# Prompt attention of a hybrid encoder layer: the probability-times-value products turned round, on two column halves of the array, four tiles at a time

## Chip, cores, metric

One core of one Trainium2 chip. The metric is the device time of one execution in microseconds (us). Engines: PE is TensorE (PEld its weight loads), DVE is VectorE, ACT is ScalarE, POOL is GpSimd, SP is SyncE, which here only issues DMAs.

## What is computed

The kernel computes one encoder layer for two token batches with shared weights, a prompt of 1024 tokens (called A in the code, `T.n` = 8 blocks of 128) and a sample of 512 (called B, `T.n` = 4). A layer has an RMS norm, one wide input projection, a bidirectional mLSTM branch, a dilated window attention branch, and two output projections. The change is in the attention branch alone, cut here to its core:

```python
A_PATTERNS = ((128, 1), (512, 4), (2048, 16))     # (window, dilation), 3 groups x 8 heads x 64
# per group: keys gathered by stride, blocks of 64 queries, 128 + 64 keys in the window
logits = einsum('bghnqe,bghnke->bghnqk', qr, kb) + bias
logits = where(mask, logits, -inf)
mx = max(logits, -1); p = exp(logits - mx[..., None]); den = sum(p, -1)
o = einsum('bghnqk,bghnke->bghnqe', p, vb)        # unnormalised
# the three groups are then mixed, weighted by exp(mx) and den
```

## The kernel before

The program runs in stages: projections of A, mLSTM of A, attention of A, mLSTM of B beside the mix of A's groups, attention of B, and the last projections. From the mLSTM of A on, the order of instructions on PE and on SP is the order in which the code issues them; on DVE, ACT and POOL a scheduler sets it at build time, by the times that it computes. Each engine executes its instructions in that order.

Between its own steps each of these stages issues dense products of another part of the layer. They come from `Fill` (L116); `fill(1)` issues about the next share of them. Their weights are loaded by DMA into `wraw` (in the attention of A by POOL), split by ACT into a high part `wh` (L274) and by DVE into a low part `wl` (L280), and multiplied in three passes by `mm3` (L211 to L213). `split_w` puts these splits behind the last attention steps in `self.held`.

Attention works on one pair of heads of one group at a time: `attend` (L1429) goes through 12 such pairs, and `attention` (L1322) cuts each into `n` tiles of 128 queries. There are three kinds of tiles. In groups 0 and 1 (dilations 1 and 4) of the prompt a tile has two key blocks of 128 (`nk` = 2), 44 tiles in all; at the ends of a sequence two half tiles of 64 queries are put together, each with one key block (`ends`, 20 tiles); in group 2 a tile has one key block (32 tiles). That makes 96 tiles for A.

A tile has four steps. `products` (L1366) multiplies queries and keys into the PSUM bank `lg`. `softmax` adds the bias and takes the maximum on DVE (L1386), negates it (L1388), and takes exponentials on ACT, with their sums (L1390). `turn` transposes the probabilities on PE into the bank `pt` (L1397) and copies them to `pts` in SBUF, on ACT (L1400) for every second tile, on DVE (L1402) for the others. `output` (L1405) multiplies: the weights of the array are the 128 x 128 probabilities, and 64 columns of values stream, for each head and key block (L1418; in an end tile the values of both blocks stream as 128 columns, L1411). The result has queries on partitions; ACT copies it from the bank `o` into the row buffer `ot` (L1420, L1414), which also holds the sums and maxima in columns 128 to 131 (`OW` = 132), and `put` (L217) queues the DMA store to `og`, issued on SP three rounds later by `tick` (L233).

The steps of consecutive tiles are interleaved. A round, `att_round` (L1490), issues these, `age` being how many rounds ago a tile began:

```python
for age, stage in ((0, 0), (1, 1), (2, 2), (None, None), (3, 3)):
    if age is None:
        fill(1)
    elif age < len(tiles) and tiles[-1 - age] is not None:
        tiles[-1 - age][stage]()
```

So PE gets, in each round: `lg` of the newest tile, transposes of the one two rounds older, dense products, and the PV products of the one three rounds older. All operands of the PV products are plain f32. `Rot` (L92) hands out row buffers in turn: ten `ot` for A. Each PSUM bank name has two buffers.

Of the kernel before, what the change touches and what calls it, by code (L numbers as in the profile page):

```python
# [22 lines left out]
F32 = mybir.dt.float32  # L23
F32R = mybir.dt.float32r
AF = mybir.ActivationFunctionType
# [4 lines left out]
P = 128  # L30
D = 1024
KT = D // P
BLK = 512
# [10 lines left out]
OW = 132  # L44
# [139 lines left out]
class Net:  # L184
# [1137 lines left out]
    def attention(self, T, u, qkv, bias, sb, ps):  # L1322

        nc = self.nc
        g, pr = divmod(u, 4)
        S, n, dil = T.S, T.n, min(DILS[g], T.n)
        L = S // dil
        wide = L > P
        W = 256 if wide else P
        q, k, v = qkv  # L1330
        c0 = 128 * (pr % 2)

        def table(c):
            b = bias()[:, :2 * W].rearrange("p (h w) -> p h w", h=2)
            j = 8 * CASES.index((g, dil)) + 2 * pr
            for hh in range(2):
                e = self.erow[j + hh]
                self.queue(("table", u), None, b[:, hh],
                           bass.AP(tensor=e.tensor, offset=e.offset + 257 - c - W, ap=[[1, P], [1, W]]))
            return b[:, :, ::-1]  # L1340


        og = T.og[:, g, pr]
        tiles, H = [], 64
        early, late = slice(H, P), slice(0, H)
# [12 lines left out]

        def stages(turned, qp, kp, kt, bt, dst, ends):
            nk = 1 if ends else len(kt)  # L1360
            W = nk * P
            pair = slice(kt[0], kt[-1] + 1, max(kt[-1] - kt[0], 1))
            qs = slice(qp, qp + P)
            ts = {}

            def products():  # L1366
                lg = self.bank("lg")
                if wide:
                    ts["lg"] = [lg[:, 0], lg[:, 1]]
                    for hh in range(2):  # L1370
                        for z in (k[hh], k[2 + hh]):
                            nc.tensor.matmul(lg[:, hh], q[hh][:, qs], z.rearrange("p (n j) -> p n j", j=P)[:, pair],  # L1372
                                             start=z is k[hh], stop=z is not k[hh])
                else:
                    kk = [z[:, kt[0]].rearrange("p a j -> p (a j)") for z in k]
                    ts["lg"] = [lg[:, 0, :P], lg[:, 0, P:2 * P]]
                    self.mm3(lg[:, 0], (q[0][:, qs], q[1][:, qs]), kk, True, True)

            def softmax():
                ls = ts["ls"] = sb.tile([P, 2, W], F32, name="ls", bufs=3)  # L1380
                ot = ts["ot"] = self.ot()
                nm = sb.tile([P, 2], F32, name="nm", bufs=3)
                blocks = [(late, slice(P, 2 * P), slice(0, P)), (early, slice(0, P), slice(P, 2 * P))]
                for hh in range(2):
                    for rows, of, by in blocks if ends else [(slice(0, P), slice(0, W), slice(0, W))]:
                        nc.vector.tensor_tensor_reduce(out=ls[rows, hh], in0=ts["lg"][hh][rows, of], in1=bt[rows, hh, by], scale=1.0,  # L1386
                                                       scalar=NEG, op0=OP.add, op1=OP.max, accum_out=ot[rows, 130 + hh:131 + hh])
                nc.vector.tensor_scalar(nm, ot[:, 130:132], -1.0, None, op0=OP.mult)  # L1388
                for hh in range(2):
                    self.held = self.held[-3:] + [nc.scalar.activation(ls[:, hh], ls[:, hh], AF.Exp, bias=nm[:, hh:hh + 1],  # L1390
                                                                      accum_out=ot[:, 128 + hh:129 + hh])]

            def turn():
                pp = self.bank("pt")
                for hh in range(2):
                    for x in range(nk):
                        nc.tensor.transpose(pp[:, hh * nk + x], ts["ls"][:, hh, x * P:(x + 1) * P], self.ident)  # L1397
                pt = ts["pt"] = sb.tile([P, 4, P], F32, name="pts", bufs=2)[:, :2 * nk]
                if turned:
                    last = nc.scalar.activation(pt, pp[:, :2 * nk], AF.Copy)  # L1400
                else:
                    last = nc.vector.tensor_copy(pt, pp[:, :2 * nk])  # L1402
                self.held = self.held[-3:] + [last]

            def output():  # L1405
                pt, ot = ts["pt"], ts["ot"]
                po = self.bank("o").rearrange("p a b -> p (a b)")
                vh = lambda x, hh: v[:, x, c0 + hh * 64:c0 + hh * 64 + 64]
                if ends:
                    for hh in range(2):  # L1410
                        nc.tensor.matmul(po[:, hh * P:hh * P + P], pt[:, hh], vh(pair, hh), start=True, stop=True)  # L1411
                    by = po[:, :2 * P].rearrange("p (h x e) -> p h x e", h=2, x=2)
                    for x, rows in enumerate((early, late)):
                        last = nc.scalar.activation(ot[rows, :128].rearrange("p (h e) -> p h e", h=2), by[rows, :, x], AF.Copy)  # L1414
                else:
                    for hh in range(2):
                        for x in range(nk):
                            nc.tensor.matmul(po[:, hh * 64:hh * 64 + 64], pt[:, hh * nk + x], vh(kt[x], hh), start=x == 0,  # L1418
                                             stop=x == nk - 1)
                    last = nc.scalar.activation(ot[:, :128], po[:, :128], AF.Copy)  # L1420
                self.held = self.held[-3:] + [last]
                for p0, cnt, row, stp in dst:
                    self.put(("og", S), og[row:row + (cnt - 1) * stp + 1:stp], ot[p0:p0 + cnt], ot)

            return products, softmax, turn, output

        return [stages(i % 2, *x) for i, x in enumerate(tiles)]

    def attend(self, T, fill, steps, first, banks, outs, after=None, beside=None, at=()):  # L1429

# [2 lines left out]
        nc = self.nc  # L1433
        self.lag = 3
        with ExitStack() as st:
# [3 lines left out]
            make = lambda b: ps.tile(shape[b], F32, name=b, bufs=2)  # L1439
            spare = {b: make(b) for b in banks}  # L1440
            self.bank = lambda b: spare.pop(b) if b in spare else make(b)
            self.ot = Rot(self, [sb.tile([P, OW], F32, name=f"ot{i}", bufs=1) for i in range(outs)])
            tables = self.pool(st, "bias" + T.name, 1, "right")
            bias = Rot(self, [tables.tile([P, BLK], F32, name=f"bias{i}", bufs=1) for i in range(4)])
            if T.n > 4:
                tables.tile([P, 2560], F32, name="apart", bufs=1)
            tiles = []
            fill.stage(steps, 12 * T.n)

# [12 lines left out]
            for i in range(12):  # L1462
                now = coming
                for j, t in enumerate(now):
# [13 lines left out]
                    self.att_round(tiles, fill)  # L1478
                    if len(tiles) in at:
                        next(beside, None)  # L1480
            for _ in range(3):
                self.tick()
                tiles.append(None)
                self.att_round(tiles, fill)
# [4 lines left out]

    def att_round(self, tiles, fill):  # L1490

        for age, stage in ((0, 0), (1, 1), (2, 2), (None, None), (3, 3)):
            if age is None:
                fill(1)
            elif age < len(tiles) and tiles[-1 - age] is not None:
                tiles[-1 - age][stage]()


# [269 lines left out]
STEPS = (316, 260, 192, 290, 86)  # L1768


def body(tc, a):
    N = Net(tc, a)
    nc = tc.nc
    (x1, y1), (x2, y2) = a["runs"]
    with ExitStack() as st:
# [145 lines left out]
        with ExitStack() as s1:  # L1921
# [30 lines left out]
            def hold(name, make):  # L1952
                def go():
                    kept[name] = make()
                return go

            with ExitStack() as s2:
# [11 lines left out]
                with ExitStack() as s3:  # L1969
                    N.gate_sums(B, N.pool(s3, "sums", 1, "right"))  # L1970
                    lanes = N.lanes(B, N.pool(s3, "lane2", 1, "right"), lambda: N.bank("o").rearrange("p a b -> p (a b)"), True)
                    N.attend(A, fill, STEPS[1], kept["qkv"], ("pt", "o", "lg"), 10, hold("head", lambda: N.ml_load(B, 0)),
                             lanes, range(44, 96, 8))
                    for _ in lanes:
                        pass
                    N.close()
# [90 lines left out]
```

## Time and profile before

| | us |
|---|---|
| median of 3 executions | 2236.45 |
| lowest, highest | 2235.32, 2239.72 |
| profiled execution, its time | 2236.86 |
| profiled execution, its span | 2235.1 |
| granted TensorE clock, mean | 0.998 |
| PE busy | 2218.1 (99%) |
| DVE busy | 1523.7 (68%) |
| ACT busy | 1120.3 (50%) |
| POOL busy | 715.7 (32%) |

In the profile each instruction has a start and a length. Lengths of PE's products overlap, since a product's results leave the array while the next one streams; how long a product holds the array is read from the distance between two starts. In a group, "xN" is the number of records, and a plain f32 product has two records, a float32r one has one. After `|` stand busy time, the mean of one in ns and idle time before it, with what ended it; in a timeline that stands in square brackets. The shape behind a product's name is first rows * columns of the weights, then what streams (partitions x columns).

### The profile page before, as it was taken

The numbers are of one execution on the slowest core, as the hardware profiler recorded it, in microseconds if no ns is written. First come the engines' busy times: TensorE is split into PE (matmuls) and PEld (weight loads), VectorE is DVE, ScalarE is ACT, GpSimd is POOL, SyncE is SP. The second block draws the span as 40 slices with busy tenths as digits, with TensorE's granted clock in tenths as the row PEclk, the third lists the DMA queues.
The fourth block names the chain that finished last, engine by engine and source line by source line (L and its number), as shares of the span: only waits on it lengthen the run. The fifth ranks groups of instructions, "written<-read, shape, count | busy, mean of one in ns | idle before, by whom it ended". The sixth has DMA issues, their size and how long they took to land.

```text
span 2235.1 us, 34988 instructions
## 1 busy us (share of the span) xinstructions
PE 2218.1 (99%) x11962; PEld 1939.6 (87%) x11962; DVE 1523.7 (68%) x2989; ACT 1120.3 (50%) x2394; POOL 715.7 (32%) x988
## 2 busy tenths in 40 slices
PE   9999999999999999999999999999999999999998
PEld 8999888888888888888888889989888888888887
DVE  7775667687776665558887765555689855665674
ACT  7332343344444343456776655656666644554332
POOL 1000423333333222236677620011165522221221
PEclk9999999999999999999999999999999999999999
DMA  3742444433323223385754779997678887776663
GB/s 124 192 115 81 174 155 165 165 141 113 113 105 112 85 85 122 114 279 173 236 186 157 191 200 247 260 250 210 208 242 289 259 261 236 236 255 201 232 233 113
DMA packets 217661, 408.81 MB, mean 183 GB/s; under 512 B 24938, under 2 KB 128042, under 8 KB 217483
## 3 DMA queue, kind: packets, MB, share of 16 engines
q1 hardware_dynamic: 187784, 298.51, 42.7%
q0 software_dynamic: 26096, 95.47, 13.7%
q10 hardware_dynamic: 3602, 12.59, 1.4%
q8 instruction: 95, 1.56, 0.3%
q14 instruction: 84, 0.68, 0.1%
HBM read 286.75 MB, written 119.73 MB: 182 GB/s over the span
## 4 chain that ended last, share of the span: by engine, by line
PE 94%; issue 2%; DMA 2%; DVE 1%; ACT 1%; POOL 0%; SPq 0%; DVEq 0%; POOLq 0%; ACTq 0%
PE d L213 14%; PE d L211 14%; PE d L212 14%; PE dense L211 12%; PE dense L213 12%; PE dense L212 12%; PE o L1418 3%; PE pt L1397 2%; PE lg L1372 2%; PE num L213 1%; PE num L211 1%; PE num L212 1%; PE a L1088 1%; PE kv L211 1%; PE kv L212 1%
## 5 line engine op out<-in xcount | busy, mean ns | idle before, releaser
L211 PE MATMUL dense<-H,wh 128*128 128x512 f32 x664 | 270.3, 407 | 0.0
L213 PE MATMUL dense<-H,wl 128*128 128x512 f32 x664 | 260.6, 392 | 0.0
L212 PE MATMUL dense<-H,wh 128*128 128x512 f32 x664 | 260.4, 392 | 0.0
L212 PE MATMUL d<-Hl,phla 128*128 128x512 f32 x608 | 236.5, 389 | 0.0
L213 PE MATMUL d<-Hh,phla 128*128 128x512 f32 x608 | 236.5, 389 | 0.0
L211 PE MATMUL d<-Hh,phla 128*128 128x512 f32 x608 | 236.5, 389 | 0.0
L280 DVE TENSOR_TENSOR wl<-wraw,wh 128x1024 fp32r<-128x1024 f32 (+1 forms) x121 | 150.0, 1240 | 72.8 <-ACT wh L274 72.5
L1386 DVE CUSTOM_DVE_ANT_0 ls<-lg,bias 128x256 f32<-128x256 f32 (+2 forms) x336 | 103.0, 332 | 116.5 <-PE lg L1372 55.4
L211 PE MATMUL d<-Hh,phlb 128*128 128x512 f32 x456 | 177.4, 389 | 0.0
L212 PE MATMUL d<-Hl,phlb 128*128 128x512 f32 x456 | 177.4, 389 | 0.0
L213 PE MATMUL d<-Hh,phlb 128*128 128x512 f32 x456 | 177.4, 389 | 0.0
L1390 ACT ACTIVATE ls<-ls,nm 128x128 f32<-128x128 f32 (+1 forms) x288 | 124.8, 435 | 92.7 <-DVE nm L1388 58.9
L274 ACT ACTIVATE wh<-wraw 128x1024 fp32r<-128x1024 f32 (+1 forms) x124 | 128.5, 1036 | 77.0 <-PE dense L212 26.1
L213 PEld LDWEIGHTS dense<-H,wl 128*128 128x128 f32 x664 | 124.7, 188 | 28.0
L695 POOL TENSOR_TENSOR psum_w<-pw_raw 128x512 f32<-128x512 f32 x38 | 58.5, 1540 | 278.4 <-DMA pw_raw<-w_in 259.6
L213 PE MATMUL d<-vhi,Hl 128*128 128x322 f32 x448 | 140.5, 314 | 0.5 <-DVE Hl L431 0.3
L211 PE MATMUL d<-vhi,Hh 128*128 128x322 f32 x448 | 140.3, 313 | 0.1
L212 PE MATMUL d<-vlo,Hh 128*128 128x322 f32 x448 | 139.6, 312 | 0.0
L212 PEld LDWEIGHTS dense<-H,wh 128*128 128x128 f32 x664 | 125.3, 189 | 14.3
L211 PEld LDWEIGHTS dense<-H,wh 128*128 128x128 f32 x664 | 125.1, 188 | 14.4
L213 PEld LDWEIGHTS d<-Hh,phla 128*128 128x128 f32 x608 | 114.2, 188 | 23.7
L211 PEld LDWEIGHTS d<-Hh,phla 128*128 128x128 f32 x608 | 114.2, 188 | 23.6
(574 smaller groups left out, 6105.0 us busy)
## 6 DMA issues: line engine op xcount, KB each, us to landing
pw_raw<-w_in SPq DMA_DIRECT2D x76, 512.0 KB, 4.1
wraw<-w_in SPq DMA_DIRECT2D x64, 512.0 KB, 4.6
aqk_a<-pwk SPq DMA_DIRECT2D x48, 512.0 KB, 3.5
aqk_b<-sw SPq DMA_DIRECT2D x48, 256.0 KB, 6.2
wraw<-w_pm POOLq DMA_DIRECT2D x24, 512.0 KB, 6.0
wraw<-w_out POOLq DMA_DIRECT2D x24, 512.0 KB, 3.9
wraw<-w_v POOLq DMA_DIRECT2D x22, 430.0 KB, 6.9
qk_a<-pwk SPq DMA_DIRECT2D x16, 512.0 KB, 2.7
```

The costliest lines, as they stand in the source:

```text
L211: nc.tensor.matmul(out, lh, rh, start=start, stop=False, **kw)
L212: nc.tensor.matmul(out, lh, rl, start=False, stop=False, **kw)
L213: nc.tensor.matmul(out, ll, rh, start=False, stop=stop, **kw)
L274: high = nc.scalar.activation(hi[:, :n], raw[:, :n], AF.Copy)
L280: low = (self.lows or nc.vector).tensor_sub(lo[:, :n], raw[:, :n], hi[:, :n].bitcast(F32))
L695: self.nc.gpsimd.tensor_add(s[:, 0], ws[1][:, 0], ws[1][:, 1])
L1088: nc.tensor.matmul(p[:, c - c0], kT[:, ct, c * P:(c + 1) * P], qT[:, ct, c * P:(c + 1) * P], start=ct == 0, stop=ct == 1)
L1372: nc.tensor.matmul(lg[:, hh], q[hh][:, qs], z.rearrange("p (n j) -> p n j", j=P)[:, pair], start=z is k[hh], stop=z is not k[hh])
L1386: nc.vector.tensor_tensor_reduce(out=ls[rows, hh], in0=ts["lg"][hh][rows, of], in1=bt[rows, hh, by], scale=1.0, scalar=NEG, op0=OP.add, op ...
L1390: self.held = self.held[-3:] + [nc.scalar.activation(ls[:, hh], ls[:, hh], AF.Exp, bias=nm[:, hh:hh + 1], accum_out=ot[:, 128 + hh:129 + hh])]
L1397: nc.tensor.transpose(pp[:, hh * nk + x], ts["ls"][:, hh, x * P:(x + 1) * P], self.ident)
L1418: nc.tensor.matmul(po[:, hh * 64:hh * 64 + 64], pt[:, hh * nk + x], vh(kt[x], hh), start=x == 0, stop=x == nk - 1)
```

## The change

For the prompt alone (`by_four`, `n > 4`) the PV products are turned round. The weights are now 64 columns of values, and the 128 columns of transposed probabilities stream; the output has the 64 channels of a head on partitions. Head 0 writes to partitions 0 to 63 and so uses columns 0 to 63 of the array, head 1 uses the other half of both. The products of four consecutive tiles are issued together, in `columns`, in the round in which the fourth tile's `output` stood, into one bank `o`. One ACT copy brings the bank to SBUF (`oT`); in the next round, behind that round's `lg` products and transposes and ahead of its dense products, `back` transposes the four tiles on PE into a bank `pt`, one ACT copy brings them to the row buffer, and the four tiles' stores are queued together. A row buffer holds four tiles, and there are four of them instead of ten; `pts` has six buffers instead of two; one closing round is added. An end tile uses four products with 64 streaming columns each instead of two. The sample's attention is unchanged. A spacer tile `apart` in SBUF shrinks.

```diff
+        by_four = n > 4
...
             def softmax():
                 ls = ts["ls"] = sb.tile([P, 2, W], F32, name="ls", bufs=3)
-                ot = ts["ot"] = self.ot()
+                if not by_four:
+                    ot = ts["ot"] = self.ot()
+                else:
+                    if slot == 0:
+                        batch["of"] = self.ot()
+                    ot = batch["of"].rearrange("p (t w) -> p t w", w=OW)[:, slot]
...
-                pt = ts["pt"] = sb.tile([P, 4, P], F32, name="pts", bufs=2)[:, :2 * nk]
+                pt = ts["pt"] = sb.tile([P, 4, P], F32, name="pts", bufs=6 if by_four else 2)[:, :2 * nk]
+                batch[slot] = (pt, kt, ends, dst)
...
+            def columns():
+                if slot < 3:
+                    return
+                po = self.bank("o").rearrange("p a b -> p (a b)")
+                vh = lambda x, hh: v[:, x, c0 + hh * 64:c0 + hh * 64 + 64]
+                for t in range(4):
+                    pt, kt, ends, _ = batch[t]
+                    of = lambda hh, a, b: po[hh * 64:hh * 64 + 64, t * P + a:t * P + b]
+                    for x in range(len(kt)):
+                        for hh in range(2):
+                            if ends:
+                                a, b = ((H, P), (0, H))[x]
+                                nc.tensor.matmul(of(hh, a, b), vh(kt[x], hh), pt[:, hh, a:b], start=True, stop=True)
+                            else:
+                                nc.tensor.matmul(of(hh, 0, P), vh(kt[x], hh), pt[:, hh * len(kt) + x], start=x == 0,
+                                                 stop=x == len(kt) - 1)
+                oT = batch["oT"] = sb.tile([P, BLK], F32, name="oT", bufs=2)
+                self.held = self.held[-3:] + [nc.scalar.activation(oT, po, AF.Copy)]
+
+            def back():
+                if slot < 3:
+                    return
+                pb = self.bank("pt")
+                for t in range(4):
+                    nc.tensor.transpose(pb[:, t], batch["oT"][:, t * P:(t + 1) * P], self.ident)
+                of = batch["of"]
+                ot = of.rearrange("p (t w) -> p t w", w=OW)
+                self.held = self.held[-3:] + [nc.scalar.activation(ot[:, :, :P], pb, AF.Copy)]
+                for t in range(4):
+                    for p0, cnt, row, stp in batch[t][3]:
+                        self.put(("og", S), og[row:row + (cnt - 1) * stp + 1:stp], ot[p0:p0 + cnt, t], of)
+
+            if by_four:
+                return products, softmax, turn, columns, back
             return products, softmax, turn, output
...
-            self.ot = Rot(self, [sb.tile([P, OW], F32, name=f"ot{i}", bufs=1) for i in range(outs)])
+            self.ot = Rot(self, [sb.tile([P, (4 if T.n > 4 else 1) * OW], F32, name=f"ot{i}", bufs=1) for i in range(outs)])
...
-                tables.tile([P, 2560], F32, name="apart", bufs=1)
+                tables.tile([P, 640], F32, name="apart", bufs=1)
...
-            for _ in range(3):
+            for _ in range(4 if T.n > 4 else 3):
...
-        for age, stage in ((0, 0), (1, 1), (2, 2), (None, None), (3, 3)):
+        for age, stage in ((0, 0), (1, 1), (2, 2), (4, 4), (None, None), (3, 3)):
```

More of the change, by code (lines that the diff above doesn't have):

```diff
@@ L1357, in attention, with stages @@
                 tiles.append((t * P, t * P, (t,), b0, [(0, P, t, dil)], False))
-        def stages(turned, qp, kp, kt, bt, dst, ends):
+        def stages(turned, slot, batch, qp, kp, kt, bt, dst, ends):
             nk = 1 if ends else len(kt)
@@ L1423, in output @@
                     self.put(("og", S), og[row:row + (cnt - 1) * stp + 1:stp], ot[p0:p0 + cnt], ot)
+            def columns():
[30 more added lines that the diff above has]
+                return products, softmax, turn, columns, back
             return products, softmax, turn, output
-        return [stages(i % 2, *x) for i, x in enumerate(tiles)]
+        batches = [{} for _ in range(n // 4)]
+        return [stages(i % 2, i % 4, batches[i // 4], *x) for i, x in enumerate(tiles)]
     def attend(self, T, fill, steps, first, banks, outs, after=None, beside=None, at=()):
@@ L1490, in att_round @@
     def att_round(self, tiles, fill):
-        for age, stage in ((0, 0), (1, 1), (2, 2), (None, None), (3, 3)):
+        for age, stage in ((0, 0), (1, 1), (2, 2), (4, 4), (None, None), (3, 3)):
             if age is None:
                 fill(1)
-            elif age < len(tiles) and tiles[-1 - age] is not None:
+            elif age < len(tiles) and tiles[-1 - age] is not None and stage < len(tiles[-1 - age]):
                 tiles[-1 - age][stage]()
@@ L1971, in body @@
                     lanes = N.lanes(B, N.pool(s3, "lane2", 1, "right"), lambda: N.bank("o").rearrange("p a b -> p (a b)"), True)
-                    N.attend(A, fill, STEPS[1], kept["qkv"], ("pt", "o", "lg"), 10, hold("head", lambda: N.ml_load(B, 0)),
+                    N.attend(A, fill, STEPS[1], kept["qkv"], ("pt", "o", "lg"), 4, hold("head", lambda: N.ml_load(B, 0)),
                              lanes, range(44, 96, 8))
```

## The prediction

> **What bounds the kernel now.** I read the page's busy times and its chain first, then the stage that the change touches, the prompt's attention (about 1305 to 1618 us), as one stretch of the table by stretches, then single rounds of it in the timeline of PE.
>
> ```profile
> PE 2218.1 (99%) x11962; PEld 1939.6 (87%) x11962; DVE 1523.7 (68%) x2989; ACT 1120.3 (50%) x2394; POOL 715.7 (32%) x988
> PE 94%; issue 2%; DMA 2%; DVE 1%; ACT 1%; POOL 0%; SPq 0%; DVEq 0%; POOLq 0%; ACTq 0%
> ```
> ```profile
> 1300.00:1620.00 320.00, 316.55 (x2058) 298.94 (x2057) 180.56 (x722) 200.29 (x658) 30.43 (x60) 0.99 0.88 234
> ```
> TensorE is busy for 99% of the span and is 94% of the chain. The second fence has, after the stretch and its length, the busy time of PE, PEld, DVE, ACT and POOL, the clock, the DMA share and GB/s: here too PE works 316.55 of 320 us, while ACT works 200 and DVE 181. The dense products that `fill` puts between the attention steps leave PE no gap, so a microsecond of PE time saved or added in this stage moves the end by about as much.
>
> **What a PV product costs today.** One round with two key blocks, as PE sees it (start, length, engine, line):
>
> ```profile
> 1399.68 0.36 PE L212 MATMUL dense<-wl,H 128*128 128x430 f32 x1
> 1399.88 0.36 PE L213 MATMUL dense<-wh,H 128*128 128x430 f32 x1
> 1400.07 1.00 PE L1418 MATMUL o<-K,pts 128*128 128x64 f32 x8
> 1400.88 0.36 PE L1372 MATMUL lg<-V1a,Q 128*128 128x256 f32 x1
> 1401.08 0.28 PE L1372 MATMUL lg<-V1b,Q 128*128 128x256 f32 x1
> 1401.20 0.28 PE L1372 MATMUL lg<-V1a,Q 128*128 128x256 f32 x1
> 1401.32 0.28 PE L1372 MATMUL lg<-V1b,Q 128*128 128x256 f32 x1
> 1401.44 0.60 PE L1397 MATMUL pt<-ident,ls 128*128 128x128 f32 x4
> 1401.79 0.44 PE L211 MATMUL dense<-wh,H 128*128 128x430 f32 x1
> 1402.08 0.35 PE L212 MATMUL dense<-wl,H 128*128 128x430 f32 x1
> ```
> ```profile
> L1418 PE MATMUL o<-K,pts x480: 217/275/294, 1320.1 to 1618.0; 128*128 128x64 f32 x160
> ```
> ```profile
> L1411 PE MATMUL o<-K,pts x80: 270/275/422, 1344.1 to 1528.4; 128*128 128x128 f32 x80
> ```
> Durations overlap, so I cost by starts. Each plain f32 product shows as two records, two passes over the array; the tile's four products are the "x8". From the last dense start (1399.88) to the second `lg` start (1401.08) are 1.20 us. Without the passes between, that would be one dense step (1399.68 to 1399.88, 0.20) and one `lg` step (1401.08 to 1401.20, 0.12). So eight passes cost 0.88 us, 0.11 each, although only 64 columns stream in each. The prompt's attention has 480 + 80 = 560 such passes: 560 x 0.11 = **61.6 us removed**.
>
> **The price of a turned pass.** The weights become 64 columns of `v`, and 128 columns of `pt` stream. The rate of an f32 pass is seen where 512 columns stream against narrow weights; the second row, from the groups by form, ends in the mean of one in ns:
>
> ```profile
> 184.76 1.05 PE L355 MATMUL d<-oh,tb 128*32 128x512 f32 x2
> ```
> ```profile
> L355 PE MATMUL d<-oh,tb 128*32 128x512 f32 x2 | 1.0, 604 | 0.0
> ```
> The pair takes 1.05 us and one takes 0.60, so starts are 0.45 apart: 0.11 for 128 columns, 0.055 for 64. The changed tiles have 480 passes of 128 columns (44 tiles with two blocks, 8 passes each; 32 with one block, 4 each) and 160 of 64 (20 end tiles, 8 each). One after the other that is 480 x 0.11 + 160 x 0.055 = 61.6 us: nothing saved. The change pays only if the two heads' halves stream at once. No row here shows two products side by side, so this term lies between 61.6 and about half. I take the half: 26.4 for the wide passes, 8.8 for the narrow ones, whose weights (64 columns at half the 0.11 of 128) take as long as their stream, and 0.11 x 24 batches = 2.6 for the pass that begins alone: **37.8 us added**.
>
> The Trainium skill (TensorE: Matmul & The Clock Gate, Part 3) measured three column tiles at 2.38 times one, not 3; an estimate at that efficiency makes the wide passes about 33 us instead of 26.4 and the forecast about 2250. No run here shows it.
>
> **Changing the array's division.** The only place where one narrow pair sits in a dense stream is this:
>
> ```profile
> 140.23 0.31 PE L212 MATMUL d<-vlo,Hh 128*128 128x322 f32 x1
> 140.38 0.31 PE L213 MATMUL d<-vhi,Hl 128*128 128x322 f32 x1
> 140.62 0.21 PE L981 MATMUL d<-ident,l_u 64*1 64x64 f32 x1
> 140.67 0.21 PE L982 MATMUL d<-ident,l_tt 64*1 64x64 f32 x1
> 140.81 0.42 PE L211 MATMUL d<-vhi,Hh 128*128 128x322 f32 x1
> 141.07 0.32 PE L212 MATMUL d<-vlo,Hh 128*128 128x322 f32 x1
> ```
> A dense step is 0.15. Going in takes 0.24 (0.09 more); coming out 0.14 after a stream of 0.05 (0.09 more); the first dense product then needs 0.26 (0.11 more), its weights no longer loaded in the shadow. With 0.055 for the first 64 weights, a batch pays 0.35, and 24 batches **8.4 us**. Going in and out at no cost is the lower bound.
>
> **Turning back.** In the round above four transposes (1401.44 to 1401.79) take 0.35 and push the dense step after them from 0.20 to 0.29 (1401.79 to 1402.08): 0.44. 24 batches: **10.6 us**.
>
> Array time together, with overlap: 37.8 + 8.4 + 10.6 - 61.6 = **-4.8 us**.
>
> **The wait that is new.** Today nothing on PE needs the copy behind a PV product (L1420, L1414), it only goes to the store. Now PE's transposes back need the ACT copy `oT`, one round step later, and PE is in order: the dense products of `fill(1)` stand behind them. From the start of the last column pass, `back` is reached after 0.11 (stream) + 0.09 + 0.11 (coming out) + 4 x 0.12 (`lg`) + 4 x 0.11 (turn) = 1.2 us; 1.0 if the turned tile has one block of each head, 0.9 in the third group (three `lg` steps, two transposes). The copy is ready after 0.27 (one pass of L1411) + 0.04 + 0.58 (below) = 0.9 us, if ACT is free. It often is not:
>
> ```profile
> 1398.78 0.58 ACT L1400 ACTIVATE pts<-pt 128x512 f32<-128x512 f32 x1
> ```
> ```profile
> 1320.07 1.00 PE L1418 MATMUL o<-K,pts 128*128 128x64 f32 x8
> ```
> ```profile
> 1321.10 0.28 ACT L1420 ACTIVATE ot<-o 128x128 f32<-128x128 f32 x1 [0.71 <-PE o L1418]
> ```
> ```profile
> 1486.84 0.50 PE L1411 MATMUL o<-K,pts 128*128 128x128 f32 x3
> ```
> ```profile
> 1490.79 0.92 ACT L274 ACTIVATE wh<-wraw 128x860 fp32r<-128x860 f32 x1 [5.25 <-DMA wraw<-w_v]
> 1491.74 0.56 ACT L1414 ACTIVATE ot<-o 64x128 f32<-64x128 f32 x2
> ```
> ```profile
> 1617.72 0.55 PE L1418 MATMUL o<-K,pts 128*128 128x64 f32 x4
> ```
> ```profile
> 1618.31 0.28 ACT L1420 ACTIVATE ot<-o 128x128 f32<-128x128 f32 x1 [2.02 <-PE o L1418]
> ```
> These are the first, one of the worst and the last of 96. The first copy begins 0.03 after the product's end (1321.07), the last 0.04 after it (1618.27), one of the two worst 4.40 after it (1487.34), because ACT stood 5.25 us in front of a weight split whose DMA was late. Over all 96 the lags add to about 58 us; every fourth, where a batch would end, adds to 20.9, and less a slack of 0.2 each to about 17. Five of those lie together between 1430 and 1490 and have one cause: counting only the worst, since PE's own wait lets ACT catch up, leaves about 10. I take **+10 us** (bounds 1 and 17).
>
> A wait can cost more than itself:
>
> ```profile
> 1493.57 1.19 PE L1397 MATMUL pt<-ident,ls 128*128 128x128 f32 x4 [2.07 <-ACT ls L1390]
> ...
> 1495.26 0.56 PE L213 MATMUL dense<-X,H 128*128 128x430 f32 x1
> 1495.62 0.56 PE L211 MATMUL dense<-wh,H 128*128 128x430 f32 x1
> ```
> After 2.07 us of idle PE the dense step is 0.36 instead of 0.20 for some microseconds. The Trainium skill (the same page, Part 1) puts the fall of the clock behind an idle window of about 3.4 us; the trace has it after 2.07. By the page no wait forecast here would slow the clock; by the row one or two may, which lies inside the bounds.
>
> **The smaller parts.** Three rounds of four lose their PV part, 0.88 or 0.45 us, so exponentials have less time before their transposes; the fence above holds the only long wait of this kind, so I add 1 us (0 to 3). One more closing round, with `back` right behind `oT`: about 0.7. Six `pts` buffers replace two because four tiles are held; PE waits on none. Stores are as many and as large, but four to six stand together on SP behind the round's loads. Four `ot` buffers of four tiles hold 16 tiles against 10, so a store has longer to land; I cost this at nothing, and if a load behind the burst came late, the price would be a wait like the 2.07 above. ACT gets two 0.58 copies per batch for four to six of 0.28, no work of weight.
>
> Sum: -4.8 + 10 + 1 + 0.7 = +6.9. The profiled execution took 2236.86 (span 2235.1), the median 2236.45; so **2243 us**, slower by 0.3%. From no change a measurement of this kernel can tell about 0.2%, 4.5 us.
>
> **Rivals.** (a) *Overlap, and ACT in time*: `oT` stands early enough in ACT's order, weights load in both halves at once so that the narrow passes halve too (-4.4). -4.8 - 4.4 + 1.7 gives 2229; without the second gain 2233. For it: the scheduler orders ACT anew around `oT`, and half of the 96 copies begin within 0.25 us. Against: the lags above. It decides if the waits at `back` stay under about 1 us in all. The Trainium skill (TensorEngine Tiling, Key Properties) says that different tiles load and multiply in parallel, which is this case; no row shows it. (b) *The halves run one after the other*: 61.6 + 8.4 + 10.6 - 61.6 = +19.0, some 6 of waits (ACT has longer to catch up) and 1.7: 2263. For it: f32 passes in two records per head come as a, a, b, b, and no row shows overlap. (c) *Half overlap*, if there is one spare set of weights for both halves: each pair of passes takes a stream and a load, 0.165, so 480 x 0.0825 + 11.4 = 51, +8.4 with the rest, +11.7: 2256. (d) *No load in the shadow at all*: +0.055 on all 640 passes over (b), 2298. Against it: L1418's eight passes at 0.11 each leave no room for load plus stream of 0.165. The Trainium skill (TensorE: Matmul & The Clock Gate, Part 3) has loads overlapping a running product only where the row group differs; the trace contradicts it.
>
> **Numbers.** Forecast 0.45 (2235 to 2252), (a) 0.18, (b) 0.24, (c) 0.10, (d) 0.03. Faster by over 0.2%: most of (a), 0.17. Within 0.2%: the rest of (a) and a quarter of the forecast, 0.15. Slower: 0.68. The range, 2229 to 2264, leaves out (d), the outer half of (b) and of (a).
>
> **What would show it.** In the trace after: starts of the column passes 0.055 apart on average (overlap) or 0.11 (none); 0.09 and 0.11 lost at each end of a batch; "pt<-ident,oT" idle on "ACT oT" for about 10 us in all, most of it around the late weights. I am wrong if that idle time is near nothing, or if the passes do not pair.

## The result and the profile after

The changed kernel takes 2249.48 us (median of 4 executions, 2244.92 to 2251.58) against 2235.89 before: ratio 1.0056, 95% interval 1.0035 to 1.0076. It is slower by 0.6%. The profiled execution is the shortest of the four, 2244.92 us with a span of 2243.2, so the traces show 8.1 us of difference (2235.1 to 2243.2). What the other three executions spend more, 4 to 7 us, no trace shows; the record has only their mean granted clocks, 0.996, 0.995 and 0.994 from the shortest to the longest, against 0.996 in the profiled one.

The busy times and the shares of the chain (the work that ended last, followed back from the end), from the page of the kernel after:

```profile
PE 2211.5 (99%) x12138; PEld 1918.7 (86%) x12138; DVE 1523.2 (68%) x2989; ACT 1120.1 (50%) x2326; POOL 712.4 (32%) x988
PE 87%; issue 4%; DMA 4%; ACT 1%; DVE 1%; POOL 1%; SPq 0%; DVEq 0%; POOLq 0%; ACTq 0%
```

PE works 6.6 us less than before and the span is 8.1 us longer, so PE stands still some 15 us more. Its share of the chain falls from 94% to 87%. The stretch of the attention of A in the table by stretches (stretch, length, busy time of PE, PEld, DVE, ACT, POOL, clock, DMA share, GB/s):

```profile
1300.00:1620.00 320.00, 303.30 (x2198) 272.74 (x2197) 176.23 (x717) 197.96 (x586) 29.39 (x58) 0.98 0.87 233
```

PE was busy 316.55 of these 320 us before, and now 303.30. ACT and DVE do no more work than before. The longest of PE's waits in this stage, before and after (PE's tile and line, then the engine, tile and line it waited for, us in all, times, longest):

```profile
PE pt L1397 <- ACT ls L1390: 2.1, 1, 2.1
```
```profile
PE pt L1456 <- ACT oT L1449: 16.3, 7, 6.2
```

The second is the new wait of `back` for the copy of the columns, 16.3 us. How it comes about is seen around one batch, first in the timeline of PE, then in that of ACT:

```profile
1403.63 0.35 PE L213 MATMUL dense<-wh,H 128*128 128x430 f32 x1
1403.92 1.97 PE L1446 MATMUL o<-pts,K 128*64 128x128 f32 x32
1405.81 0.39 PE L1373 MATMUL lg<-V1a,Q 128*128 128x256 f32 x1
1406.04 0.28 PE L1373 MATMUL lg<-V1b,Q 128*128 128x256 f32 x1
...
1406.39 0.60 PE L1403 MATMUL pt<-ident,ls 128*128 128x128 f32 x4
1410.02 0.66 PE L1456 MATMUL pt<-ident,oT 128*128 128x128 f32 x4 [3.02 <-ACT oT L1449]
1410.43 0.44 PE L211 MATMUL dense<-wh,H 128*128 128x430 f32 x1
1410.71 0.47 PE L212 MATMUL dense<-wl,H 128*128 128x430 f32 x1
1410.97 0.56 PE L213 MATMUL dense<-wh,H 128*128 128x430 f32 x1
1411.33 0.56 PE L211 MATMUL dense<-X,H 128*128 128x430 f32 x1
```
```profile
1404.27 0.19 ACT L1396 ACTIVATION_READ_ACCUMULATOR ls<-ls,nm 128x1 f32 x1
1408.56 0.92 ACT L274 ACTIVATE wh<-wraw 128x860 fp32r<-128x860 f32 x1 [4.10 <-DMA wraw<-w_v]
1409.38 0.58 ACT L1449 ACTIVATE oT<-o 128x512 f32<-128x512 f32 x1
1409.86 0.59 ACT L1407 ACTIVATE pts<-pt 128x512 f32<-128x512 f32 x1
```

The columns are done at 1405.89. ACT would be free, but the next instruction in its order is a weight split that waits for its DMA until 1408.56; `oT` stands behind it. In the kernel before, where ACT's copy went only to a store, a late weight load shows in PE's waits through the exponentials alone (the one wait of 2.1 us above). Now it holds PE through `oT`, and the dense products stand behind the waiting transposes in PE's order. After the wait the dense step is 0.36 (1410.97 to 1411.33) where 0.20 is usual.

### The profile page after: what moved, and what is told of

Read it like the earlier page. It is cut to its first block, busy times and chain, and to the rows that moved or that the text cites. A ratio compares the mean times of both kernels' runs of the same rounds, so it can differ in the third digit from the quotient of the medians.

```text
span 2243.2 us, 35157 instructions
## 1 busy us (share of the span) xinstructions
PE 2211.5 (99%) x12138; PEld 1918.7 (86%) x12138; DVE 1523.2 (68%) x2989; ACT 1120.1 (50%) x2326; POOL 712.4 (32%) x988
## 4 chain that ended last, share of the span: by engine, by line
PE 87%; issue 4%; DMA 4%; ACT 1%; DVE 1%; POOL 1%; SPq 0%; DVEq 0%; POOLq 0%; ACTq 0%
PE d L213 14%; PE d L211 14%; PE d L212 14%; PE dense L211 11%; PE dense L213 11%; PE dense L212 11%; DMA wraw<-w_v 2%; PE num L213 1%; PE num L211 1%; PE num L212 1%; PE pt L1403 1%; PE a L1088 1%; PE o L1425 1%; PE kv L211 1%; PE kv L212 1%
## 5 line engine op out<-in xcount | busy, mean ns | idle before, releaser
L274 ACT ACTIVATE wh<-wraw 128x1024 fp32r<-128x1024 f32 (+1 forms) x124 | 128.4, 1036 | 69.7 <-PE dense L212 21.7
L211 PEld LDWEIGHTS d<-Hh,phla 128*128 128x128 f32 x608 | 114.1, 188 | 23.7
L212 PEld LDWEIGHTS d<-Hl,phla 128*128 128x128 f32 x608 | 114.1, 188 | 23.7
```

The costliest lines, as they stand in the source:

```text
L211: nc.tensor.matmul(out, lh, rh, start=start, stop=False, **kw)
L212: nc.tensor.matmul(out, lh, rl, start=False, stop=False, **kw)
L274: high = nc.scalar.activation(hi[:, :n], raw[:, :n], AF.Copy)
```

## The experiments

To compare kernels I read PE's starts in each trace. The stage of A's attention is taken from the first `lg` to the first product behind the last attention step. For each product I took the distance to the next start; its bare distance is the lower quartile of the distances between the same neighbours on both sides (same shapes) over the kernels, and its own distance within the column products. Summed, the bare distances are "array"; what is left is "waits", which includes slow dense steps behind an idle time. Numbers are good to some tenths. Where `back` comes behind the dense products or a round later (e2, e3 and what builds on e3), nine more dense products (about 2 us) fall before the stage's end and as many fewer behind it. Each row rests on one execution, while the ratio is of medians: the traces of the kernel after, e5, e6, e7 and e12 are of their shortest execution (e5's is 5.5 us below its median), those of e2 and e9 of their longest.

| kernel | ratio to before (95%) | stage | array | waits | of which back; turn; lg; dense |
|---|---|---|---|---|---|
| before | 1 | 308.5 | 298.7 | 9.8 | -; 3.0; 1.4; 1.4 |
| after | 1.0056 (1.0035 to 1.0076) | 314.4 | 287.1 | 27.3 | 18.3; 1.4; 2.0; 2.8 |
| e1_older | 1.0017 (1.0007 to 1.0028) | 310.2 | 286.7 | 23.5 | 1.3; 12.0; 6.1; 2.2 |
| e2_after_dense | 1.0035 (1.0024 to 1.0046) | 314.3 | 288.5 | 25.8 | 10.9; 1.7; 5.7; 5.2 |
| e3_round_later | 1.0004 (0.9995 to 1.0013) | 308.0 | 288.4 | 19.5 | 2.5; 6.5; 7.3; 0.7 |
| e4_by_head | 1.0086 (1.0071 to 1.0101) | 325.2 | 310.7 | 14.5 | 9.4; 0.7; 0.4; 1.5 |
| e5_loads_early | 1.0039 (1.0026 to 1.0052) | 310.7 | 288.4 | 22.2 | 2.3; 12.8; 2.2; 2.5 |
| e8_stores_apart | 1.0018 (1.0008 to 1.0027) | 310.2 | 288.4 | 21.8 | 3.9; 8.2; 4.5; 2.8 |
| e6_half_weights | 0.9968 (0.9957 to 0.9980) | 296.7 | 288.4 | 8.3 | 1.0; 4.7; -; 0.1 |
| e7_before_half | 0.9976 (0.9966 to 0.9987) | 301.3 | 298.7 | 2.5 | - |
| e9_closing | 1.0018 (1.0009 to 1.0028) | 308.2 | 288.4 | 19.8 | 1.8; 8.3; 3.4; 4.0 |
| e10_third_raw | 1.0018 (1.0007 to 1.0029) | 306.3 | 288.4 | 17.9 | -; 9.1; 4.6; 1.8 |
| e11_before_third | 0.9983 (0.9973 to 0.9992) | 302.7 | 298.7 | 4.0 | -; 0.0; -; - |
| e12_after_third | 1.0034 (1.0021 to 1.0047) | 308.8 | 287.1 | 21.7 | 2.7; 5.7; 9.0; 1.9 |

The change thus takes 11.6 us off the array's work and adds 17.5 us of waits. The theory to be tested: the wait of `back` for `oT` is the loss, it comes from late weight DMAs in front of ACT's copy, and without it the array's gain is kept. The rivals: the halves do not really overlap; or the wait only holds the place of others, because loads, ACT and DVE cannot keep up with a faster PE in this stage.

**e1_older: the transposes back take an older batch's copy.** `back` reads the `oT` of the batch before, which has long been there.

```diff
-                oT = batch["oT"] = sb.tile([P, BLK], F32, name="oT", bufs=2)
+                oT = batch["oT"] = sb.tile([P, BLK], F32, name="oT", bufs=3)
...
+                older, self.older = getattr(self, "older", batch["oT"]), batch["oT"]
...
-                    nc.tensor.transpose(pb[:, t], batch["oT"][:, t * P:(t + 1) * P], self.ident)
+                    nc.tensor.transpose(pb[:, t], older[:, t * P:(t + 1) * P], self.ident)
...
-                tables.tile([P, 640], F32, name="apart", bufs=1)
+                tables.tile([P, 128], F32, name="apart", bufs=1)
```

> Leaves out part of the computation: the transposes back read the copy of the batch before, so each batch's rows hold an older batch's values. All instructions stay in place; only PE's wait for the fresh copy goes. Theory 1 (the change shortens PE's own work by some 13 us in this stage and loses it, and more, in the wait for oT, 18.2 us in the profile): about 2228 us, faster than the kernel before by 0.3 to 0.5%, and PE idle at the transposes back under 1 us. Theory 2 (ACT's lateness bounds the stage; a wait taken away there appears at the transposes of the probabilities or at the dense products): not under 2240 us, with 10 us or more of PE waits on ACT elsewhere.

Measured: 2239.98 us (2235.99 to 2245.43) against 2235.78 of the kernel before. PE's longest waits in the stage:

```profile
PE pt L1403 <- ACT pts L1407: 5.1, 4, 3.0
PE lg L1373 <- DMA og_a<-ot: 2.7, 2, 2.4
PE pt L1403 <- ACT ls L1396: 2.3, 5, 0.6
```

The wait at `back` is gone, from 18.3 to 1.3, and the median is 9.5 us below the kernel after. But in the trace most of it came back: 10.6 us at the transposes of probabilities, which need ACT's exponentials and its copies out of the `pt` banks, and 4.1 at `lg`, so that the stage is only 4.2 us shorter. This is what the second theory expected: the wait at `back` had also been giving those their time.

**e2_after_dense: `back` behind the round's dense products.**

```diff
-        for age, stage in ((0, 0), (1, 1), (2, 2), (4, 4), (None, None), (3, 3)):
+        for age, stage in ((0, 0), (1, 1), (2, 2), (None, None), (4, 4), (3, 3)):
```

> The transposes back stand behind the round's dense products instead of ahead of them, 1.2 to 1.8 us later on PE. Theory 1: the four long waits of the profile (6.3, 3.3, 3.2, 2.9 us) shrink by about 1.6 each and the small ones go, so some 9 us of wait are left: about 2236 us, the same as the kernel before within 0.3%. Theory 2: the waits move on, 2245 to 2250 us as for the changed kernel.

Measured: 2243.96 us (2241.69 to 2246.49). Between `columns` and `back` now lies one more share of dense products, about 1.6 us (some 800 passes of 0.2 in 100 rounds), and the wait at `back` falls only to 10.9. In the kernel after, ACT stands 3 to 5 us in front of each of the four late weight splits, so one share of dense products doesn't cover them. The time lies between the two that were expected:

```profile
PE pt L1456 <- ACT oT L1449: 10.0, 4, 4.2
```

**e3_round_later: `back` one round later.**

```diff
-            for _ in range(4 if T.n > 4 else 3):
+            for _ in range(5 if T.n > 4 else 3):
...
-        for age, stage in ((0, 0), (1, 1), (2, 2), (4, 4), (None, None), (3, 3)):
+        for age, stage in ((0, 0), (1, 1), (2, 2), (5, 4), (None, None), (3, 3)):
```

> The transposes back stand one whole round later (age 5), 2.4 to 3.6 us more for the copy; one more closing round. Theory 1: only the longest wait leaves a rest of about 3 us: about 2230 us, faster than before by 0.2 to 0.4%. Theory 2: 2245 us or more.

Measured: 2237.47 us (2235.34 to 2238.73); the interval takes in no change: it has the time of the kernel before, 7.5 us from either of the two times expected. The longest waits of PE:

```profile
PE lg L1373 <- DMA bias<-erow: 3.1, 1, 3.1
PE pt L1403 <- DVE nm L1394: 2.5, 3, 1.4
PE lg L1373 <- DMA V0b<-aqk_a: 2.0, 1, 2.0
```

A whole round of slack takes the wait for `oT` away, 18.3 to 2.5. In its place stand waits for loads that come late, and for the softmax (`nm` is the negated maximum on DVE).

**e4_by_head: all products of head 0, then all of head 1.** The same column products in another order, so that, but for the one change of head in a batch, no two neighbours lie in different halves.

```diff
-                for t in range(4):
...
-                    for x in range(len(kt)):
-                        for hh in range(2):
+                for hh in range(2):
+                    for t in range(4):
...
+                        for x in range(len(kt)):
```

> The column products of a batch go head by head: all of head 0, then all of head 1, so neighbours use the same half of the array and cannot stream at once. The rest is as in the changed kernel. Theory 1 with the overlap as the source of the gain: starts 0.11 us apart for wide passes and 0.055 for narrow ones, 480 x 0.11 + 160 x 0.055 = 61.6 us against 34.9 measured for the column passes, so +27 us less a few us of wait that the longer batches cover: about 2270 us. Theory 2 (PE is not the bound here): under 2258 us.

Measured: 2256.18 us (2255.65 to 2257.18). The column products in the groups of the kernel after, then of this one (count, busy us, mean ns):

```profile
L1446 PE MATMUL o<-pts,K 128*64 128x128 f32 x480 | 32.9, 278 | 0.0
```
```profile
L1446 PE MATMUL o<-pts,K 128*64 128x128 f32 x480 | 56.3, 278 | 0.0
L1456 PE MATMUL pt<-ident,oT 128*128 128x128 f32 x96 | 15.7, 287 | 7.6 <-ACT oT L1449 7.6
```

Same passes, same mean, but PE is busy with them for 56.3 us instead of 32.9. By starts, a batch of 32 such passes takes 3.26 us instead of 1.90, one pass every 0.109 except around the change of head. So the halves do stream at once in the kernel after, and only because their products alternate. The array grows by 23.6 us, the stage by 10.8 (the medians by 6.7). The rest was paid for by waits, which fall from 27.3 to 14.5: with slower columns ACT has more time. So the time came out as the second theory had it (under 2258), although the overlap is real: a change of PE's work in this stage is largely taken up by waiting.

**e5_loads_early and e8_stores_apart: the loads that e3 waits for.** On top of e3, e5 issues the next pair's loads in four rounds instead of seven, and e8 on top of e5 lets the four stores of a batch go out in four rounds.

```diff
-                            self.spread(T.n - 1 if i or T.n > 4 else 1)
+                            self.spread(4 if T.n > 4 else T.n - 1 if i else 1)
```
```diff
-                        self.put(("og", S), og[row:row + (cnt - 1) * stp + 1:stp], ot[p0:p0 + cnt, t], of)
+                        self.put(("og", S), og[row:row + (cnt - 1) * stp + 1:stp], ot[p0:p0 + cnt, t], of, lag=self.lag + t)
```

> The round-later version with the next pair's loads handed to SP over 4 rounds instead of 7. Its profile has 7.4 us of waits at the logits, for tables and keys of the next pair that landed late. Theory 3 (late loads are what keeps the round-later version from being faster): these waits fall to 2 us or less, about 2232 us. Theory 4 (what holds it is ACT, which stands in front of weight splits whose DMA is late): 2236 to 2239 us, as the round-later version.

> The early loads, and the four tiles' stores handed to SP in four rounds instead of one, so that no burst of five stores (4.2 us of SP's time in the round-later profile) stands ahead of loads. Theory 3 with the burst as a cause: 2 us or more below the version with early loads alone. Otherwise: within 1.5 us of it.

Measured: e5 2245.55 us (2240.05 to 2247.27), e8 2240.82 (2236.20 to 2245.18), against 2236.40 before. The waits at `lg` fell in e5, 7.3 to 2.2, and those at `turn` rose, 6.5 to 12.8:

```profile
PE pt L1403 <- ACT ls L1396: 4.6, 4, 1.8
PE pt L1403 <- DVE nm L1394: 3.6, 2, 3.3
```

With the loads earlier the waits only moved, and neither expectation (2232, or 2236 to 2239) was met. Why the median is 8 us above e3's is not shown: e5's trace is of an execution 5.5 us below it. By the medians, spreading the stores wins back a good half of that loss (4.7 us, where 2 or more were expected if the burst of stores has a part in it); no wait that stands out shows where.

**e6_half_weights and e7_before_half: half the weight traffic.** In A's attention each weight block loads only its first half; e6 is e3 with this, e7 the kernel before with it.

```diff
-        self.loaded = self.side.dma_start(raw[:, :kt * cols], src)
+        n = kt * cols
+        if getattr(self, "half", False):
+            n //= 2
+            src = src[:, :n]
+        self.loaded = self.side.dma_start(raw[:, :n], src)
```

> The round-later version with only the first half of each weight block loaded from memory during the prompt's attention, so the products that use the rest work on old weights (that part of the computation is wrong). All engine instructions stay; only the bytes of the weight DMAs are halved. Theory 4: ACT no longer waits for weights, the waits at the transposes (about 9 us) go, and with less traffic the late loads come sooner too: about 2227 us. Theory 3: only the logits' waits shrink somewhat, about 2234 us. Theory 1 without any of this: 2237 us.

> The kernel before with the same half loads of the weights in the prompt's attention (same part wrong). Its profile has 10 us above the bare array time in this stage, 3 of them at transposes behind a late weight. Theory 4: gains 3 to 5 us, about 2232 us, less than the round-later version gains from the same edit (about 10), since its rounds leave more time. Otherwise: no change, 2236 us.

Measured: e6 2228.80 us (2225.80 to 2232.32), e7 2230.80 (2228.46 to 2232.29). The stretch 1300 to 1630 of e6, then of e7:

```profile
1300.00:1630.00 330.00, 326.01 (x2362) 294.05 (x2361) 197.10 (x757) 217.82 (x623) 41.17 (x77) 1.00 0.85 226
```
```profile
1300.00:1630.00 330.00, 330.00 (x2154) 311.25 (x2154) 194.73 (x751) 214.94 (x687) 39.32 (x75) 1.00 0.83 220
```

These are near the 2227 and 2232 expected if late weights are the cause. With less traffic e3's waits fall from 19.5 to 8.3 and those of the kernel before from 9.8 to 2.5; in e7 PE never stops. So the late weights cost the kernel before too. Even then the changed form gains only 2 us, and the intervals overlap: the stage is 4.6 us shorter, 10.3 us of array less 5.8 us of waits, and 1.9 of it is lost again behind A's attention. There the last stage, behind the attention of B, is 2.5 us longer in e6 (146.8 against 144.3); 2.1 of these are PE's waits for DVE at the transposes `tp`, which e7 does not have. All four kernels with dense products in a fifth closing round have this stage long (e3, e5, e6, e8: 145.6 to 146.8), and all others have it at 143.9 to 144.4. How the two hang together is open.

**e9_closing: no dense products in the last closing round.** On e3.

```diff
-            for _ in range(5 if T.n > 4 else 3):
+            for x in range(5 if T.n > 4 else 3):
...
-                self.att_round(tiles, fill)
+                self.att_round(tiles, fill if x < 4 else lambda share: None)
```

> The round-later version without dense products in its fifth closing round, so the later stages begin with the same share of them as in the kernel before (in the round-later profile nine products stood earlier, and the later stages were 3 us longer). If that shift is the cause: about 2234.5 us, some 3 below the round-later version's 2237.5. If not: 2237 to 2238 us.

Measured: 2239.20 us (2236.62 to 2242.45) against 2235.86 before, no gain on e3. The edit takes away the nine products behind the last `back` (up to the next stage's first product there are 15, as in the kernel before, and 24 in e3). The nine ahead of it stay (813 in the stage, as in e3), since they belong to the fourth closing round. The last stage is 144.2 us again, but what lies between it and A's attention is 4.6 us longer than in e3; e9's trace is of its longest execution.

**e10_third_raw, e11_before_third, e12_after_third: a third buffer for raw weights.** Instead of less traffic, earlier traffic: A's attention gets a third `wraw`, so that a weight load starts one block sooner. e10 is this on e9, e11 on the kernel before, e12 on the kernel after. In e10 and e12 `pts` has five buffers instead of six, for room. The edit for e11:

```diff
-        self.done = 0
+        self.done = self.deep = 0
...
-            self.fetch(len(self.ready) + 1)
+            self.fetch(len(self.ready) + 1 + self.deep)
...
-                tables.tile([P, 2560], F32, name="apart", bufs=1)
+                extra = tables.tile([P, RING], F32, name="wraw2", bufs=1)
+                self.wraw.insert(0, extra)
+                fill.deep = 1
...
+                            self.wraw, fill.deep = [x for x in self.wraw if x is not extra], 0
```

> The same, with a third buffer for raw weights in the prompt's attention and each weight load issued one block earlier (pts with five buffers for the room). Theory 4 (late weight DMAs hold ACT, and the turned products make that dearer): the waits at the transposes fall from about 9 us to 3, about 2229 us, faster than the kernel before by 0.3%. If the DMA queues are simply full in this stage, loads issued earlier take longer and delay the others: 2233 to 2238 us.

> The kernel before with the same third buffer and earlier weight loads. Theory 4: its waits behind late weights go (3 to 5 us): about 2232 us. If the DMA queues are full: 2235 to 2237 us.

> The changed kernel, transposes back in their first place, with the third buffer and earlier weight loads. Theory 4: the long waits for oT come from ACT standing in front of late weights, so the 18 us shrink to about 6: about 2237 us. If the long waits have another cause: 2246 to 2250 us as the changed kernel.

Measured: e10 2238.72 us (2234.89 to 2245.53), e11 2231.68 (2230.15 to 2235.22), e12 2243.48 (2241.43 to 2244.26), against 2235.86. ACT's wait for `w_v` in the kernel before, in e11, in the kernel after and in e12, from 1300 on:

```profile
ACT wh L274 <- DMA wraw<-w_v: 11.7, 3, 5.2
```
```profile
ACT wh L274 <- DMA wraw<-w_v: 4.4, 1, 4.4
```
```profile
ACT wh L274 <- DMA wraw<-w_v: 12.5, 3, 5.2
```
```profile
ACT wh L274 <- DMA wraw<-w_v: 4.0, 1, 4.0
```

e11 is the fastest kernel here at full weight traffic and beats the one before and the one after; it is 0.17% below the one before (ratio 0.9983, 0.9973 to 0.9992): its waits fall from 9.8 to 4.0. In e12 the wait at `back` falls from 18.3 to 2.7, with `back` where the change put it. That shows the cause of this wait from the other side: with the weights in time (the wait that is left, at 1307.64, lies ahead of the stage), ACT's copy is in time. But the time falls only by 6 us, between the two that were expected, since PE then waits elsewhere; nor did e10 come near its 2229. Waits of e12, then the longest of e10:

```profile
PE lg L1373 <- DMA V1a<-aqk_a: 3.6, 1, 3.6
PE pt L1403 <- ACT ls L1396: 2.7, 4, 1.2
...
PE pt L1456 <- ACT oT L1449: 1.7, 3, 0.8
```
```profile
PE pt L1403 <- DVE nm L1394: 7.4, 3, 3.5
```

No turned form with full traffic came below the kernel before; the nearest is e3, at its time. So the theory holds for where the wait at `back` comes from, and fails in its last part, that without this wait the array's gain is kept; there the second rival was right.

## Why the prediction was right, point by point

The forecast of 2243 us and its direction, slower, stand; the median of 2249.48 lies inside the range and 6.5 above the forecast. The medians are 13.6 apart, twice the sum's +6.9; the two traces, 8.1 apart, are close to it. That closeness is in part luck: two terms were off by some 7 and 8 us in opposite directions.

**The halves overlap: right.** In the x32 row of the fence, 32 passes and what follows them take 1.89 us (1403.92 to 1405.81). Inside it, by the single records, passes start in pairs from the first on, 7 ns apart within a pair and 0.109 from pair to pair. In e4, where the two heads do not alternate, the pairs are gone, so a pair is one pass of each head. Rivals (b), (c) and (d) fall. The Trainium skill (TensorE: Matmul & The Clock Gate, Part 3) gives 2.38 times for three column tiles; here two gave twice, so the estimate made with its efficiency (33 us for the wide passes) was too high: 240 pairs of 0.109 are 26.2. The rule of the Trainium skill (TensorEngine Tiling, Key Properties) that different tiles load and multiply in parallel agrees with these starts.

**Column passes and the division's change, 37.8 + 8.4 = 46.2: too high by about 7.** Measured are 2.09 us for a batch of 32 passes (0.09 going in, 1.89, and 0.11 at the first `lg`), 1.88 and 1.68 for the kinds with narrow passes, 1.215 for group 2, and 39.0 for all 24. The 0.35 for each change was right (0.09 going in, 0.05 at the first pair, 0.10 behind the last, 0.11 at the first `lg`). Two parts of the 37.8 were not: the lead-in of a pass, 2.6, does not show (2.09 is 16 pairs of 0.109 and the 0.35); and the narrow passes, costed at 8.8 because their weights would not load at once, halve like the others, as rival (a) had it:

```profile
1444.86 0.66 PE L1446 MATMUL o<-pts,K 128*64 128x128 f32 x8
1445.34 0.40 PE L1444 MATMUL o<-pts,K 128*64 128x64 f32 x8
1445.58 0.61 PE L1446 MATMUL o<-pts,K 128*64 128x128 f32 x8
```

Eight narrow passes take 0.24 (1445.34 to 1445.58), 0.06 a pair. So the array gains not 4.8 but about 12 (39.0 + 10.6 - 61.6 = -12.0; 11.6 by the table).

**The wait at `back`, +10 between 1 and 17: right in kind, mis-sized.** It measures 16.3 in the view of waits and 18.3 with the short ones, at or just over the upper bound. The value 10 came from counting five late copies as one. The four long waits lie apart, at the batches behind late weights, and each was paid on its own: PE's wait did not let ACT catch up, because ACT itself stood still. ACT's idle times before the splits at 1408.56, 1451.01, 1492.88 and 1529.46 are 4.10, 5.21, 3.19 and 3.79. The sum over every fourth lag, 17, was nearer.

**What a wait costs more than itself: seen.** 2.8 us of slow dense steps in the stage, against 1.4 before. The granted clock is 0.50 from 1410.81, shortly after the wait of 3.02 us, to 1414.22, and from 1451.77, within the wait of 6.15, to 1458.60; it stays at 1.00 around those of 2.75 and 3.14. The Trainium skill (TensorE: Matmul & The Clock Gate, Part 1) puts the clock's fall behind an idle window of about 3.4 us; here it had fallen after 3.02. By that figure, too, the worst lag that the prediction lists, 4.40, was long enough for a fall, other than it says.

**The closing round, +0.7, right; short rounds, +1, not seen in the kernel after.** The last `back` waits 0.70. The waits at `turn` do not grow by 1 there, they fall from 3.0 to 1.4. But where the wait at `back` is taken away by e1, e3 or e5, the waits at `turn` are 6.5 to 12.8 us, so that wait seems to have covered them. The prediction took the terms as independent. Rival (a) had the narrow passes right, but its 2229 with the wait gone was not reached: e1 and e3, which remove it, stand at 2240 and 2237.

**"A microsecond of PE time saved or added in this stage moves the end by about as much": wrong.** The array's work fell by 11.6 us and the stage grew by 5.9; e4 adds 23.6 to the array and 10.8 to the stage. PE was busy for 99%, but what feeds it had little to spare: with half the weight traffic the waits of e3 and of the kernel before fall by 11.2 and 7.3 us (e6, e7).

**What the sum did not hold:** about 3 us behind the stage, where the next one begins. The view of waits has 1.6 of them, PE waiting for POOL, which at this place it did not before:

```profile
PE num L211 <- POOL ql L1136: 1.1, 1, 1.1
...
PE num L213 <- POOL scl L1128: 0.5, 1, 0.5
```

Right behind these waits the granted clock is 0.50 from 1639.50 to 1642.91, which it is not there in the kernel before. PE works all through these 3.41 us, so at half the clock they cost about 1.7 us more, by estimate. Together that is about the 3.

**Open.** The 5 us between the profiled and the other executions of the kernel after; the lower clock of the longest goes with it (0.994 against 0.996; 0.002 of 2249 us is 4.5 us, by estimate), but which waits came before is not recorded. Why the waits at `turn` grow in e1, e5 and e10: that exponentials have less time in rounds without PV products is argued from the waits' names and not tried by itself. Each kernel has one trace, and the table's split rests on it.

## What to carry to other kernels

Where PE is at 99%, array time saved can come back as waits, here 12 us saved and 17 us of waits; look for what is late next before costing a gain. A PE step that reads another engine's copy needs as much slack as the worst thing that can stand ahead of that copy in its engine's order, here a weight split of 3 to 5 us behind a late DMA: a whole round. A late load that costs little while nothing waits for it (the third raw buffer was worth 4 us to the kernel before) is better mended first.

## What the runs showed of the hardware beyond expectation

Plain f32 products on two column halves, issued in turn with two records each, pair fully: 7 ns apart within a pair, 0.109 us a pair of 128 columns, 0.06 a pair of 64. When the order is by head PE is busy with the same 480 passes for 56.3 us against 32.9. One excursion into the two halves and back costs about 0.35 us: 0.09 going in, 0.15 at the first and last pair, 0.11 at the first full product behind them.
